# First stage of a two-layer backbone: the first quarter's modulation fetched between the fourth and the fifth token tile and summed ahead of the last tiles' transposes, with two-bank transposes

## The chip, the cores and the metric

The kernel runs on one core of one Trainium2 chip. The metric is the device time of one execution in microseconds (us); less is better. Five engines work side by side, each through its own queue in order: PE (matrix multiplication; the profile shows its weight loads apart, as PEld), DVE (vector work), ACT (activations, casts, copies), POOL (a few small operations) and SP (which here only issues transfers from main memory, HBM). Engines wait for each other by semaphores. PE writes its results into PSUM, eight banks of 512 float32 values in each of 128 partitions; everything else lies in the on-chip memory SBUF.

## What is computed

Two layers of a diffusion backbone over 512 latent tokens and 256 context tokens of width 1024. Each sub-layer begins with an RMS norm and a modulation, a shift and a scale that are computed from a conditioning vector by a large matrix; the change lies in the very first of these and in the projection behind it:

```python
sc, scc = silu(c), silu(c_ctx)
m_lat = split((sc  @ mod_w[l] + mod_b[l])[:, None, :], 6, axis=-1)
m_ctx = split((scc @ mod_w[l] + mod_b[l])[None, None, :], 6, axis=-1)
h_ctx = rms(x_ctx, norm_pre_mix[l]) * (1 + m_ctx[1]) + m_ctx[0]
h_lat = rms(x_lat, norm_pre_mix[l]) * (1 + m_lat[1]) + m_lat[0]
# layer 0: one combined projection of both streams
gq, gk, gv, gog, gz, aq, ak, av = split(concat([h_ctx, h_lat]) @ w_in, EVEN_SIZES)
```

Behind that come gated linear attention and softmax attention, an output projection, a SwiGLU network, and a second layer of another kind. The change leaves all of these as they are.

## The kernel before

Tokens are held as six tiles of 128: tiles 0 to 3 are latent, 4 and 5 context. The order is 4, 5, 0, 1, 2, 3 throughout. The 1024 features are eight blocks of 128, k = 0 to 7. For precision every matmul operand x is split in two parts, a rounded high part xH (a cast on ACT) and the rest xL (a subtraction on DVE). A product then takes three matmuls: xH with wH, xH with wL, xL with wH (`mm3`).

The first stage is in `run`, from line 1891. Its parts:

- **Tiles** (lines 1893 to 1904). For each of the six tiles: a fetch of 512 KB on SP, the sum of squares on ACT (line 676), the reciprocal root on DVE and POOL (lines 666 and 668), a scaling on DVE (line 1897), eight 128x128 transposes on PE (line 1902) and two copies out of PSUM into `xT`, one on ACT, one on DVE (line 1904). The transposes go four at a time into a one-bank PSUM tile, of which there are two (`tr_tile`).
- **Modulation.** It is worked through in four quarters, qd = 0 to 3, of two feature blocks each. `loads(qd)` (line 1913) fetches eight pieces of 256 KB of `mod_w`, and the 2 x 288 columns of the input projection that belong to this quarter, the *z weights*; the function `unit` (line 761) also casts and subtracts those weights. `sums(qd, ks)` (line 1927) multiplies the pieces with the conditioning vectors into `mod_acc`, 32 matmuls for each half of ks.
- **Apply.** `apply(qd)` (line 1943) turns the sums by a transposition on PE (`modT`), adds the bias, forms the affine numbers A and B (line 1947), applies them to `xT` (on DVE at line 1956, on ACT at line 1954) and splits the result into high and low parts (`put`, lines 734 and 735), first for the context tokens, then for the latent ones.
- **Projection.** `z(t0, qd)` (line 1959) multiplies tiles t0 and t0 + 1 with the z weights of one quarter: 12 matmuls of 288 columns. Over four quarters each z accumulates into its place in PSUM: z(4, .) and z(0, .) into a two-bank tile each (`mm_tile`, of which there are two), z(2, .) into two one-bank tiles.

The order of PE is written out by hand (lines 1976 to 1990) and kept while `self.pinned` is set: sums and apply of the first quarter, then for each further quarter the first half of its sums, the z of the quarter before, the second half of its sums, more z, apply. ACT, DVE, POOL and SP are ordered by the scheduler when the program is built, by the order in which the program names the work and by when it expects operands to be ready. At run time each queue is strictly in order.

`even_mixer` (line 1079) goes on: z(., 3) for all tiles with the evacuation on ACT (lines 1101 to 1104), then small constants, then a long list of steps (line 1219) that begins with `qk0`, the first query and key projections of the linear attention. The first `next` of `qk0` fetches, casts and subtracts its two weight units; the second issues its first matmuls (`gqk`).

Of the kernel before, what the change touches and what calls it, by code (L numbers as in the profile page):

```python
# [8 lines left out]
F32 = mybir.dt.float32  # L9
# [8 lines left out]
P = 128  # L18
# [298 lines left out]
class Net:  # L317
# [3 lines left out]
    def __init__(self, ctx, tc, I, out):  # L321
# [5 lines left out]
        self.turns, self.steps, self.pair = [], [], []  # L327
# [433 lines left out]
    def unit(self, src, k, n, pool=None, to=None):  # L761

        nc = self.nc
        raw = self.wp.tile([P, WU], F32, tag="raw", bufs=3, name="raw")
        H, L = to or [(pool or self.wp).tile([P, WU], F32R, tag=f"w{x}", bufs=4, name=f"w{x}") for x in "HL"]
        m = k * n
        rv = raw[:, :m].rearrange("p (k n) -> p k n", k=k)
        nc.sync.dma_start(out=rv, in_=src)
        nc.scalar.copy(H[:, :m], raw[:, :m])  # L769
        nc.vector.tensor_tensor(L[:, :m], raw[:, :m], H[:, :m].bitcast(F32), op=ALU.subtract)  # L770
        return H[:, :m].rearrange("p (k n) -> p k n", k=k), L[:, :m].rearrange("p (k n) -> p k n", k=k)
# [307 lines left out]
    def even_mixer(self, h, mix, z):  # L1079
# [19 lines left out]

        self.pinned = True  # L1100
        for t0 in tiles:
            for a, pt in enumerate(z(t0, 3)):
                nc.scalar.copy(zn[:, t0 + a, :], pt[:, 0:32])
                nc.scalar.copy(q_part(0)[:, t0 + a], pt[:, 32:288].rearrange("p (m e) -> p m e", m=4))
# [37 lines left out]

        gq, gk, ends = {}, {}, {}
        def qk(c):
            Ws = {x: self.unit_cols(w, x * P) for x in (c, c + 2)}
            yield
            for x in (c, c + 2):
                pt = self.mm_tile(f"gqk{x}")
                for g in groups:
                    self.gemm_T(pt, Ws[x], h, (g,))  # L1150
                    if g is groups[-1]:
                        t = gqk[x // 2] if c == 0 else mixg.tile([P, NT], F32, tag=f"gqk{x // 2}", bufs=1, name=f"gqk{x}")
                        if x < 2:
                            nc.scalar.mul(t, pt[:, :NT], 0.125)
                            gq[c] = t
                        else:
                            nc.scalar.copy(t, pt[:, :NT])
                            gk[c] = t
                    yield
# [50 lines left out]
        running = {}  # L1210
# [660 lines left out]
    def run(self):  # L1871
# [19 lines left out]
        with self.pool("pre0") as pp:  # L1891
# [85 lines left out]
            for qd in range(4):  # L1977
                loads(qd)
# [229 lines left out]
```

## Time and profile before

| | us |
|---|---|
| median of three timed runs (1678.63 to 1679.25) | 1679.15 |
| the profiled execution: its span from first to last instruction | 1679.4 |
| PE busy in it | 1639.6 |
| DVE busy | 1313.1 |
| ACT busy | 917.3 |
| first matmul of `gqk`, where the first stage ends for PE | 54.51 |

The profiled execution's span lies 0.25 us above the median. In the timeline's rows stand the start and the length of an instruction or of a merged group, the engine, the line of the kernel, the operation, what it writes and reads, how many of them, and in brackets how long its engine was idle before it and which event ended that. SPq and ACTq are the parts of an engine's queue that issue transfers. A group's length runs from its first start to its last end. Matmuls overlap in the pipeline, so the distance between two starts says more than the length of one.

### The profile page before, as it was taken

The page shows a single profiled execution, that of the slowest core. Times are in us where ns is not written, and L with a number is a line of the kernel's source. Part 1 is how long each engine was busy: PE and PEld are TensorE (multiplying, and loading weights), DVE is VectorE, ACT ScalarE, POOL GpSimd, SP SyncE. Part 2 cuts the span into 40 slices and gives each one's busy share as a digit, 9 for nine tenths or more (in the row PEclk, how much of TensorE's full clock was granted, in tenths as well). Part 3 has the DMA queues.
Part 4 walks back from the last instruction along what each step waited for, and adds up shares of the span by engine and source line. Part 5 has one row for each costly group of instructions (what it writes and reads, how often), then busy time and mean ns, then how long its engine had stood idle before and what let it go on. Part 6 is the DMA issues. An engine that isn't in the chain of part 4 may idle for free.

```text
span 1679.4 us, 32397 instructions
## 1 busy us (share of the span) xinstructions
PE 1639.6 (98%) x13347; PEld 1474.1 (88%) x13347; DVE 1313.1 (78%) x2104; ACT 917.3 (55%) x1560; POOL 122.5 (7%) x129
## 2 busy tenths in 40 slices
PE   6999998999999999999999999999999999999998
PEld 5899987888999999997887788888888899999886
DVE  4899768976898988767668648788775499987887
ACT  4745567845543443435447536566564565555564
POOL 1004110011000000002101000000000100000310
PEclk9999999999999999999999999999999999999999
DMA  9651003164243545249516542111114334433973
GB/s 330 193 156 40 2 28 101 52 213 153 85 140 101 149 146 182 76 146 211 101 57 209 189 135 64 52 53 51 52 55 159 125 103 121 118 101 101 225 164 138
DMA packets 184735, 204.77 MB, mean 122 GB/s; under 512 B 7142, under 2 KB 141836, under 8 KB 184588
## 3 DMA queue, kind: packets, MB, share of 16 engines
q1 hardware_dynamic: 173632, 181.82, 34.5%
q0 software_dynamic: 9024, 17.30, 6.0%
q10 hardware_dynamic: 1932, 3.59, 0.6%
q8 instruction: 104, 1.70, 0.4%
q14 instruction: 43, 0.35, 0.1%
HBM read 193.23 MB, written 9.46 MB: 121 GB/s over the span
## 4 chain that ended last, share of the span: by engine, by line
PE 80%; DVE 9%; DMA 4%; ACT 4%; issue 2%; POOL 1%; SPq 0%; DVEq 0%; ACTq 0%; POOLq 0%
PE nat L355 12%; PE a L355 10%; PE ff L355 8%; PE E L355 7%; PE oproj L355 6%; PE x L355 5%; PE o L355 4%; PE b L355 3%; PE D L355 3%; PE fq L355 3%; PE gqk L355 2%; PE pearly L355 2%; PE q L355 2%; PE S L355 2%; PE poh L355 1%
## 5 line engine op out<-in xcount | busy, mean ns | idle before, releaser
L355 PE MATMUL nat<-wH,x 128*128 128x256 f32 (+2 forms) x968 | 226.2, 322 | 3.1 <-ACT x L734 2.6
L355 PEld LDWEIGHTS nat<-wH,x 128*128 128x128 f32 x968 | 162.0, 190 | 21.2 <-ACT x L734 4.2
L824 ACT CAST wH<-raw 128x1024 fp32r<-128x1024 f32 x120 | 124.8, 1051 | 101.3 <-DVE raw L849 39.3
L825 DVE TENSOR_TENSOR wL<-raw,wH 128x1024 fp32r<-128x1024 f32 x120 | 145.8, 1222 | 24.2 <-ACT wH L824 23.7
L355 PE MATMUL nat<-wL,x 128*128 128x256 f32 (+2 forms) x484 | 153.5, 317 | 1.8 <-DVE wL L770 1.8
L770 DVE TENSOR_TENSOR wL<-raw,wH 128x1024 fp32r<-128x1024 f32 (+1 forms) x83 | 98.7, 1199 | 50.5 <-ACT wH L769 49.5
L355 PE MATMUL ff<-x,wH 128*128 128x512 f32 (+1 forms) x512 | 127.7, 340 | 0.0
L769 ACT CAST wH<-raw 128x1024 fp32r<-128x1024 f32 (+1 forms) x83 | 84.8, 1031 | 73.3 <-PE ff L355 19.6
L668 POOL TENSOR_TENSOR rs<-ms,neghalf 128x1 f32<-128x1 f32 (+2 forms) x62 | 64.2, 1040 | 789.7 <-DVE ms L666 789.5
L355 PE MATMUL oproj<-wH,x 128*128 128x512 f32 x320 | 102.2, 395 | 0.7 <-ACT x L1290 0.7
L355 PEld LDWEIGHTS nat<-wL,x 128*128 128x128 f32 x484 | 92.1, 190 | 7.8 <-DVE wL L770 2.7
L355 PEld LDWEIGHTS ff<-x,wH 128*128 128x128 f32 x512 | 87.3, 190 | 10.0
L597 DVE SCALAR_TENSOR_TENSOR macc<-mraw,scT,macc 128x1024 f32<-128x1024 f32 x70 | 88.0, 1282 | 10.0 <-DMA mraw<-in_mod_w_dram 9.6
L355 PE MATMUL x<-wH,two 128*128 128x512 f32 x280 | 90.7, 393 | 1.2 <-DVE y L1803 0.7
L976 ACT COPY qkh<-arr 128x512 f32<-128x512 f32 x112 | 70.1, 643 | 36.6 <-DVE arr L981 32.5
L1725 POOL DMA_DIRECT2D t<-in_ffn_w_down_dram x36 | 41.8, 1199 | 640.4 <-DVE t L1764 341.0
L355 PE MATMUL ff<-x,wL 128*128 128x256 f32 (+1 forms) x256 | 86.2, 337 | 0.0
L849 DVE TENSOR_TENSOR raw<-raw 128x512 f32<-128x512 f32 x120 | 82.8, 690 | 2.8
L981 DVE TENSOR_TENSOR arr<-arr,f 128x512 f32<-128x512 f32 x112 | 74.3, 689 | 2.1 <-ACT qkh L976 0.3
L355 PEld LDWEIGHTS oproj<-wH,x 128*128 128x128 f32 x320 | 59.9, 188 | 13.3 <-ACT x L1290 1.3
L355 PE MATMUL E<-T,wH 128*128 128x384 f32 (+1 forms) x320 | 70.4, 309 | 0.3 <-DVE go L902 0.3
L355 PE MATMUL E<-x,wH 128*128 128x384 f32 (+1 forms) x320 | 70.7, 310 | 0.0
(420 smaller groups left out, 4531.1 us busy)
## 6 DMA issues: line engine op xcount, KB each, us to landing
mraw<-in_mod_w_dram SPq DMA_DIRECT2D x80, 512.0 KB, 4.0
raw<-in_ffn_w_gate_dram SPq DMA_DIRECT2D x44, 512.0 KB, 4.9
raw<-in_ffn_w_up_dram SPq DMA_DIRECT2D x44, 512.0 KB, 4.5
raw<-in_odd_w_in_dram SPq DMA_DIRECT2D x40, 512.0 KB, 3.8
t<-in_ffn_w_down_dram POOLq DMA_DIRECT2D x30, 512.0 KB, 8.0
raw<-in_ffn_w_down_dram SPq DMA_DIRECT2D x28, 512.0 KB, 6.4
mraw<-in_mod_w_dram SPq DMA_DIRECT2D x32, 256.0 KB, 6.4
raw<-in_even_w_in_dram SPq DMA_DIRECT2D x16, 512.0 KB, 6.8
```

Source lines behind the costliest of these rows:

```text
L355: return self.pin(self.nc.tensor.matmul(*a, **k))
L597: nc.vector.scalar_tensor_tensor(a, u, w, a, op0=ALU.mult, op1=ALU.add)
L668: nc.gpsimd.tensor_tensor(rs, ms, self.neghalf.to_broadcast([P, w]), op=ALU.pow)
L769: nc.scalar.copy(H[:, :m], raw[:, :m])
L770: nc.vector.tensor_tensor(L[:, :m], raw[:, :m], H[:, :m].bitcast(F32), op=ALU.subtract)
L824: self.nc.scalar.copy(H, f)
L825: self.nc.vector.tensor_tensor(L, f, H.bitcast(F32), op=ALU.subtract)
L849: add = lambda o, x, y: nc.vector.tensor_tensor(o, x, y, op=ALU.add)
L976: nc.scalar.copy(qkv[:, :, :, half, :], dst)
L981: nc.vector.tensor_tensor(dst, dst, tb, op=ALU.mult)
L1725: add = lambda o, src: self.pin(nc.gpsimd.dma_start(out=o, in_=src, accum_op=ALU.add))
```

## The change

Four things are done in the first stage, and one behind it.

1. The tile loop becomes two functions, `fetch` and `turn`, so that the fetches can be named apart from the rest. The transposes of a tile go into one two-bank tile (`mm_tile`) instead of two one-bank tiles.
2. SP's order becomes tiles 4, 5, 0, 1, then `loads(0)`, then tiles 2, 3, then `loads(1)` to `loads(3)`. PE's written order begins with the transposes of four tiles; then come the sums of the first quarter, and the transposes of tiles 2 and 3 between the first z.
3. `unit` is cut in two: `fetched` issues the transfer and returns the function that casts and subtracts. The z weights of a quarter are now cast and subtracted by `weights(qd)`, which names them after the context half of that quarter's apply, and `behind` keeps them, on ACT and on DVE, behind the last cast and subtraction of that half.
4. `apply` is cut into `cols` (affine numbers) and `apply` for one stream and a range of tiles; in the first quarter the latent half is applied in two parts.
5. In `even_mixer` the weights of `qk0` are named ahead of the last z, behind the last cast and subtraction of the last apply; the evacuations of z on ACT are kept behind the first of these casts.

```diff
     def unit(self, src, k, n, pool=None, to=None):
+        return self.fetched(src, k, n)(pool, to)
+
+    def fetched(self, src, k, n):
         nc = self.nc
         raw = self.wp.tile([P, WU], F32, tag="raw", bufs=3, name="raw")
         m = k * n
-        nc.sync.dma_start(out=rv, in_=src)
-        nc.scalar.copy(H[:, :m], raw[:, :m])
-        nc.vector.tensor_tensor(L[:, :m], raw[:, :m], H[:, :m].bitcast(F32), op=ALU.subtract)
+        nc.sync.dma_start(out=raw[:, :m].rearrange("p (k n) -> p k n", k=k), in_=src)
+
+        def split(pool=None, to=None):
+            H, L = to or [(pool or self.wp).tile([P, WU], F32R, tag=f"w{x}", bufs=4, name=f"w{x}") for x in "HL"]
+            self.casts = self.casts[-1:] + [nc.scalar.copy(H[:, :m], raw[:, :m])]
+            nc.vector.tensor_tensor(L[:, :m], raw[:, :m], H[:, :m].bitcast(F32), op=ALU.subtract)
...
+        return split
...
+    @contextmanager
+    def behind(self):
+        with ExitStack() as s:
+            for x in self.latest:
+                s.enter_context(self.tc.issue_after(x.ins))
+            yield
...
+            def turn(t):
+                xt = xts.pop(t)
                 rs = self.rstd(self.sumsq(xt), D)
                 nc.vector.tensor_scalar(xt, xt, rs, None, op0=ALU.mult)
+                pt = self.mm_tile(f"xT{t}")
+                for k in range(KD):
+                    self.tr(pt[:, k * P : (k + 1) * P], xt[:, k * P : (k + 1) * P], self.ident)
                 for hf in range(2):
...
                     (nc.vector.tensor_copy if hf else nc.scalar.copy)(dst, src)
...
-                zu.append(self.unit(src, 2, 288))
+                zu.append(self.fetched(src, 2, 288))
...
+            def weights(qd):
+                with self.behind():
+                    zu[qd] = zu[qd]()
...
+            self.pinned = True
+            fetch(4, 5, 0, 1)
+            loads(0)
+            fetch(2, 3)
+            for qd in range(1, 4):
                 loads(qd)
-            self.pinned = True
+            for t in (4, 5, 0, 1):
+                turn(t)
             sums(0, range(8))
-            apply(0)
+            cols(0)
+            apply(0, 1, 4, 2)
+            weights(0)
+            turn(2)
+            apply(0, 0, 0, 2)
+            z(4, 0)
+            turn(3)
+            z(0, 0)
+            apply(0, 0, 2, 2)
             for qd in range(1, 4):
                 sums(qd, lo)
-                z(4, qd - 1)
-                if qd < 3:
-                    z(0, qd - 1)
+                if qd > 1:
+                    z(4, qd - 1)
+                    if qd < 3:
+                        z(0, qd - 1)
                 sums(qd, hi)
                 z(2 if qd < 3 else 0, qd - 1)
-                apply(qd)
+                cols(qd)
+                apply(qd, 1, 4, 2)
+                weights(qd)
+                apply(qd, 0, 0, 4)
             z(2, 2)
...
+        with self.behind():
+            early = qk(0)
+            next(early)
         self.pinned = True
-        for t0 in tiles:
-            for a, pt in enumerate(z(t0, 3)):
...
+        with self.tc.issue_after(self.casts[0].ins):
+            for t0 in tiles:
+                for a, pt in enumerate(z(t0, 3)):
...
```

`issue_after(x)` keeps what is named inside it behind the instruction x in x's queue; it adds no semaphore.

More of the change, by code (lines that the diff above doesn't have):

```diff
@@ L1 @@
-from contextlib import ExitStack
+from contextlib import ExitStack, contextmanager
 import concourse.bass as bass
@@ L326, in __init__ @@
         self.pinned = False
-        self.turns, self.steps, self.pair = [], [], []
+        self.turns, self.steps, self.pair, self.casts = [], [], [], []
         pool = lambda name, bufs=1, **k: ctx.enter_context(tc.tile_pool(name=name, bufs=bufs, **k))
@@ L1141, in ev_kv @@
             nc.scalar.copy(natk[:, t0 : t0 + 2, :], pt[:, :, :256])
[L1143 to L1159, printed above, removed]
         def values(c):
@@ L1209, in even_mixer @@
         att = Attention(self, natq, natk, cat)
-        running = {}
+        running = {"qk0": early}
         def run(steps):
```

62 lines of the change are left out of this document (38 added, 24 removed).

## The prediction

> **What bounds the kernel now.** The page comes first, then the busy time by stretch, then the timeline of the first stage, engine by engine. The page gives the profiled execution's span, and the view by stretch (length; busy us and instructions of PE, PEld, DVE, ACT and POOL; granted clock; DMA share; GB/s) splits its beginning.
>
> ```profile
> span 1679.4 us, 32397 instructions
> ...
> 0.00:16.00 16.00, 6.49 (x27) 5.33 (x28) 6.27 (x15) 9.72 (x17) 5.31 (x15) 1.00 0.92 324
> 16.00:36.00 20.00, 16.91 (x239) 14.01 (x237) 11.80 (x32) 9.16 (x17) 0.00 (x0) 1.00 1.10 354
> 20.36:54.51 34.15, 30.65 (x406) 26.66 (x406) 19.96 (x56) 16.58 (x37) 0.52 (x1) 1.00 0.91 281
> 54.51:219.00 164.49, 164.33 (x2310) 150.67 (x2308) 142.16 (x297) 94.91 (x186) 27.25 (x21) 1.00 0.28 85
> ```
>
> The span of 1679.4 us is 0.25 us above the median of the three timed runs, 1679.15 us. From 54.51, where the first qk matmul starts, to 219 PE is busy for 164.33 of 164.49 us. So whatever the first stage gains or loses at 54.51 is handed on whole: up to 219 PE has no gap that could take it up. Behind 219 PE waits now and then for DVE and ACT, whose work there follows from PE's own; I take the shift to pass through these waits too, which no row here proves. The stage itself is loose: 30.65 of 34.15 us. The change touches only what lies before 54.51, so the question is when the matmul that now stands at 54.51 will start. In PE's timeline (start, us, instruction, idle time before it and its releaser) the turning points of the stage are:
>
> ```profile
> 8.08 1.91 PE L358 MATMUL xT<-ident,xt 128*128 128x128 f32 x8
> 16.88 1.10 PE L358 MATMUL xT<-ident,xt 128*128 128x128 f32 x8 [0.27 <-DVE xT L1904]
> 20.36 1.96 PE L355 MATMUL mod_acc<-mraw,scT 128*32 128x128 f32 x64
> 24.97 0.40 PE L355 MATMUL nat<-wH,x 128*128 128x288 f32 x1 [0.84 <-ACT x L734]
> 31.27 0.27 PE L358 MATMUL modT<-ident,modrows 128*128 128x128 f32 x1
> 33.33 0.40 PE L355 MATMUL nat<-wH,x 128*128 128x288 f32 x1 [0.78 <-ACT x L734]
> 37.38 1.08 PE L355 MATMUL mod_acc<-mraw,scT 128*32 128x128 f32 x32
> 38.39 0.40 PE L355 MATMUL nat<-wH,x 128*128 128x288 f32 x1
> 38.63 0.30 PE L355 MATMUL nat<-wL,x 128*128 128x288 f32 x1
> 40.10 0.27 PE L358 MATMUL modT<-ident,modrows 128*128 128x128 f32 x1
> 42.16 0.40 PE L355 MATMUL nat<-wH,x 128*128 128x288 f32 x1 [0.78 <-ACT x L734]
> 44.14 1.08 PE L355 MATMUL mod_acc<-mraw,scT 128*32 128x128 f32 x32
> 46.86 0.27 PE L358 MATMUL modT<-ident,modrows 128*128 128x128 f32 x1
> 48.92 0.40 PE L355 MATMUL nat<-wH,x 128*128 128x288 f32 x1 [0.21 <-ACT x L734]
> 54.51 0.71 PE L355 MATMUL gqk<-x,wH 128*128 128x512 f32 x2
> ```
>
> Eight transposes take 1.91 us early and 1.10 us later. The first quarter's modulation sums (mod_acc) start at 20.36 and take 1.96. One z, a pair of tiles in one quarter, is 12 matmuls: from 38.39 to the transposition modT at 40.10, 1.71 us, of which 1.47 follow the start of its second matmul at 38.63 (the first that reads wL). Half a quarter's sums take 1.01 (37.38 to 38.39). I use three marks: M1, M2 and M3, the ends of the modT of the second, third and fourth quarters: 31.54, 40.37 and 47.13. What PE then waits for is ACT's first cast of x (the brackets at 33.33 and 42.16: 0.78 us each).
>
> ```profile
> 11.86 0.68 DVE L1904 COPY xT<-xT 128x512 f32<-128x512 f32 x1
> 23.55 0.17 DVE L1947 SCALAR_TENSOR_TENSOR aff<-modcol,col 128x4 f32<-128x4 f32 x1
> 26.18 0.67 ACT L769 CAST wH<-raw 128x576 fp32r<-128x576 f32 x1
> 31.97 0.17 DVE L1947 SCALAR_TENSOR_TENSOR aff<-modcol,col 128x4 f32<-128x4 f32 x1
> 32.17 0.81 ACT L1954 ACTIVATE xT<-xT,modcol,aff 128x512 f32<-128x512 f32 x1 [5.33 <-DVE aff L1947]
> 32.89 1.22 ACT L734 CAST x<-xT 128x256 fp32r<-128x256 f32 x3
> L770 DVE TENSOR_TENSOR wL<-raw,wH 128x576 fp32r<-128x576 f32 x4 | 3.0, 751 | 0.0
> ```
>
> These are ACT's and DVE's rows. The quarter's affine numbers are ready at 23.72 in the first quarter and at 32.14 in the second, 0.60 after M1. ACT first runs a latent activation (0.81), then the three casts (1.22 for two context casts and one latent one). The cast of the z weights for the second quarter (0.67, and 0.75 for DVE's part) stands at 26.18, 7 us ahead of the z that reads it (33.33), in time that nobody waits for.
>
> **The change, part by part.**
>
> *Transfers.* The order on SP becomes four tiles, the first quarter's modulation, its z weights, two tiles, the rest.
>
> ```profile
> mraw<-in_mod_w_dram SPq DMA_DIRECT2D x32, 256.0 KB, 6.4
> xt<-in_x_dram SPq DMA_DIRECT2D x4, 512.0 KB, 5.6
> raw<-in_even_w_in_dram SPq DMA_DIRECT2D x4, 288.0 KB
> ```
>
> The count of bytes is the same. By the rates above (324 GB/s to 16 us, 354 after) 5.18 MB are in by 16 us. Four tiles and eight blocks of 256 KB are 4.2 MB: in by about 13.2 instead of 16.2. The fifth tile (0.52 MB) follows at about 15.5, with 0.3 MB of z weights ahead of it, the sixth at 17.0, and everything after that lands when it did: the second quarter at about 23, the fourth at about 37 (12.5 MB). No later sum comes to wait for it, as the first wants its data after 23 and the last after 40.
>
> *First quarter.* Now the sums stand behind four tiles' transposes, not six. Turn 4 still runs at 8.08 to 9.99, turn 5 follows to 11.9 without a wait, as there are two double banks. Turn 0 needs the first one back, so it waits for DVE's copy that ends at 12.54; at the early pace it ends at 14.5, turn 1 at 15.6 to 16.4; I take 16.0. The sums add 1.96: 18.0. From sums to affine it takes 1.40 (22.32 to 23.72), so the affine numbers stand at **A = 19.4** instead of 23.72. Ends: 17.5, if the copy comes right behind its transposes and the rest runs at 1.10; 21.2, if the sums run at the early pace too.
>
> From A the two context casts and, held behind them now, the weights' cast and subtraction have to run. In the second quarter's rows the context casts end 1.35 after the affine numbers (32.14, activation, 32.89, two of three casts); with the shorter first activation I take 1.05. With 0.67 and 0.75 behind, the second matmul of z(4, 0) starts at A + 2.5. Meanwhile the fifth tile is normalised:
>
> ```profile
> L676 ACT ACTIVATE junk<-xt 128x1024 bf16<-128x1024 f32 x6 | 6.3, 1057 | 3.2 <-DMA xt<-in_ctx_dram 2.7 <-DMA xt<-in_x_dram 0.4
> L676 ACT ACTIVATION_READ_ACCUMULATOR junk<-xt 128x1 f32 x6 | 1.1, 188 | 0.0
> L666 DVE TENSOR_SCALAR ms<-ss 128x1 f32<-128x1 f32 x6 | 0.9, 150 | 7.4 <-ACT junk L676 7.4
> L668 POOL TENSOR_TENSOR rs<-ms,neghalf 128x1 f32<-128x1 f32 x6 | 4.3, 717 | 9.6 <-DVE ms L666 9.4
> L1897 DVE TENSOR_SCALAR xt<-xt,rs 128x1024 f32<-128x1024 f32 x6 | 4.5, 752 | 1.9 <-POOL rs L668 1.9
> ```
>
> 1.06 + 0.19 + 0.15 + 0.72 + 0.75 = 2.87 us from its landing at 15.5 to its transposes. They stand behind the first modT in PE's order, so at about 18.7 to 19.8; ACT is idle from 15.5 to A but for copies, and they hide ahead of z(4, 0). The sixth tile's do not: PE's order is fixed, and after z(4, 0) (1.47) come its transposes (1.10), then a wait of 0.75 that is new: z(0, 0) takes the double bank that those transposes filled, so DVE's 0.68 copy has to end first, z(4, 0) holding the other. Then z(0, 0) 1.71, both halves of the second sums 2.0, z(2, 0) 1.71, modT 0.27: 9.0 in all. M1 = A + 2.5 + 9.0 = **30.9, 0.6 earlier** than 31.54. Of 4.3 us gained at A, 1.4 are spent waiting on weights, and 2.9 on transposes, their copy and a half of sums that stood ahead of z before. By A's ends it is from 2.5 earlier to 1.2 later.
>
> *Other quarters.* The weights' cast is held behind the second context cast on ACT, its subtraction behind DVE's. That is a new wait. Queued behind it on ACT are the latent casts, on DVE their subtractions. After M: 0.60 to the affine numbers, 1.35 to the end of the context casts, 0.67, 0.75: the second z matmul at M + 3.4, z's end at M + 4.9.
> - Second quarter: z(0, 1) adds 1.71, so the sums that stood at 37.38 (M1 + 5.84) stand at M1 + 6.6: 0.75 later.
> - Third: the sums at 44.14 (M2 + 3.77) stand at M2 + 4.9: 1.1 later.
> - Fourth: z(0, 3) and z(2, 3) behind, so 54.51 (M3 + 7.38) becomes M3 + 8.3: 0.9 later.
>
> Sum: **2.75 later**. Nothing in before shows this queue, so both ends: if ACT takes the context casts ahead of the latent activation, each loses 0.4 less (1.5 in all); if a latent cast (0.6) goes first, 0.6 more (4.5). I take the middle, since the rows show activation, context, latent.
>
> *qk weights and evacuations.* The casts of the first qk weights now stand behind the last latent cast, and z's evacuations on ACT behind the first of them.
>
> ```profile
> L769 ACT CAST wH<-raw 128x1024 fp32r<-128x1024 f32 x2 | 2.1, 1052 | 0.0
> L770 DVE TENSOR_TENSOR wL<-raw,wH 128x1024 fp32r<-128x1024 f32 x1 | 1.2, 1215 | 0.0
> 47.21 10.37 SPq L461 DMA_DIRECT2D mraw<-in_mod_w_dram  x4
> 110.67 1.28 DVE L537 SCALAR_TENSOR_TENSOR macc<-mraw,scT,macc 128x1024 f32<-128x1024 f32 x1
> 114.99 1.06 PE L355 MATMUL mod_acc<-macc,one 128*32 128x512 f32 x8
> ```
>
> 1.05 and 1.22 are hidden by z(0, 3) and z(2, 3), 3.4 us of PE; without that cover 2.3 at most. The z weights' raw buffers come free later, so on SP two fetches of value weights, and behind them perhaps the next modulation's at 47.21, go out later. That modulation is summed on DVE to 111.95 and read by PE at 114.99: 3.0 us of slack, and more if PE comes later. I cost it at nothing; beyond the slack it would cost what the fetch is late by. The first quarter's latent half split in two adds short operations beside z(4, 0): nothing.
>
> [...] The profile grants PE a clock of 1.00 in every stretch, yet the same eight transposes take 1.91 us at 8.08 and 1.10 at 16.88: PE is slow at first and turns fast somewhere between. [...]
>
> Sum: 1679.4 - 0.6 + 2.75 = 1681.5 in the profiled execution, 0.25 less beside the median: **1681.3 us**. Ends: -2.5 + 1.5 = -1.0 and 1.2 + 4.5 = +5.7.
>
> **The rivals.**
> - **R1, slower: the fifth tile queues behind the weights on ACT.** ACT's order is a plan made ahead. If it puts that tile's sum of squares behind the weights' cast (A + 1.7 = 21.1), its transposes start 2.87 later, at 24.0, and z(4, 0) at 25.1, ends at 26.8; by the forecast it ended at 23.4. 3.4 more: 1684.7. It decides from 17.9 on: up to there the transposes are out of the way when the weights are. For it: the landing (15.5) and the casts are near each other. Against it: the slow transposes put A behind 17.5 in any case.
> - **R2, the front gain outweighs the waits.** Turns run promptly and fast (A = 17.5, -2.5) and the quarters cost 1.5 to 2.2: 0.3 to 1.0 faster, 1678.5. If the weights also slip in at no cost, 1676.6; it would take another 0.8 from somewhere to get under 1675.8. For it: before, these casts never held PE. Against it: they now cannot start before the affine numbers.
> - **R3, PE falls back to its slow pace** in the gaps between sums, turn 2 and z(4, 0): 1.91 / 1.10 on z(4, 0), turn 3 and z(0, 0) (4.5 us) adds 3.3: 1684.6. [...]
> - **R4, the change does nothing**: the scheduler's order or the transfers give the same 54.51. Transfers don't bind, so little: 1679.2.
>
> **How the numbers follow.** Forecast 0.47 (1679.8 to 1682.5 on its own), R1 0.19, R2 0.21, R3 0.07, R4 0.06. About 0.2% (3.4 us) is what a measurement can tell from no change. Forecast, R4 and most of R2 lie within it; R1 and R3 nearly all beyond it; of R2 0.06 beyond it on the fast side, for sizes that I have wrong. So faster 0.06, same 0.69, slower 0.25. The range goes from inside R2 to past R1: 1677.4 to 1685.2.
>
> **What would show it.** Right: sums near 16 to 18; the fifth tile's sum of squares before the first context cast; the weights' casts between context and latent casts in each quarter, with PE waiting on DVE's wL at each z(4, q); the sixth tile's transposes between z(4, 0) and z(0, 0) with a wait on the copy; first qk matmul near 56.6. Wrong: weights' casts early, or ACT starting the second context cast long before M + 1.7; first qk before 54; a gap on PE behind 56, which would break the handing-on.

## The result, and the profile after

The changed kernel takes **1694.18 us** (median of 4 runs, 1691.42 to 1697.02), the kernel before 1679.2 beside it (4 runs, 1678.63 to 1680.59): ratio 1.009, 95% interval 1.0076 to 1.0105. It is 15 us slower; the prediction was 1681.3, with a range up to 1685.2.

The page of the changed kernel begins:

```profile
span 1690.5 us, 32401 instructions
...
PE 1640.4 (97%) x13347; PEld 1477.7 (87%) x13347; DVE 1313.6 (78%) x2107; ACT 918.4 (54%) x1563; POOL 123.5 (7%) x129
```

PE has as much work as before (1640.4 us, 1639.6 before) and more waiting. Where it waits shows in where the same matmuls start:

| | before | after | later by |
|---|---|---|---|
| first quarter's sums begin | 20.36 | 14.53 | -5.8 |
| M1 | 31.54 | 33.15 | 1.6 |
| M2 | 40.37 | 42.89 | 2.5 |
| M3 | 47.13 | 51.00 | 3.9 |
| first `gqk` | 54.51 | 63.51 | 9.0 |
| first `oproj`, the output projection | 338.7 | 348.1 | 9.4 |
| first `a` (the feed-forward part that follows `pearly`) | 450.3 | 464.2 | 13.9 |
| first `fq`, in the second layer | 1004.2 | 1015.8 | 11.6 |
| end of the span | 1679.4 | 1690.5 | 11.1 |

Of the 13.9 us that are lost by `a`, 9.0 come ahead of `gqk` (3.9 of them up to M3) and 4.5 between `oproj` and `a`, a place that the prediction never looked at. In PE's timeline the first stage now reads (start, us, instruction, idle time before it and what ended that):

```profile
14.53 1.95 PE L355 MATMUL mod_acc<-mraw,scT 128*32 128x128 f32 x64
...
20.98 1.87 PE L358 MATMUL xT<-ident,xt 128*128 128x128 f32 x8 [3.75 <-DVE xt L1922]
...
25.06 1.03 PE L358 MATMUL xT<-ident,xt 128*128 128x128 f32 x8
27.50 0.40 PE L355 MATMUL nat<-wH,x 128*128 128x288 f32 x1 [1.40 <-DVE xT L1929]
...
32.88 0.27 PE L358 MATMUL modT<-ident,modrows 128*128 128x128 f32 x1
...
35.86 0.40 PE L355 MATMUL nat<-wH,x 128*128 128x288 f32 x1 [1.70 <-ACT wH L774]
36.66 0.40 PE L355 MATMUL nat<-wL,x 128*128 128x288 f32 x1 [0.39 <-DVE wL L775]
...
45.56 0.40 PE L355 MATMUL nat<-wH,x 128*128 128x288 f32 x1 [1.66 <-ACT wH L774]
...
53.67 0.40 PE L355 MATMUL nat<-wH,x 128*128 128x288 f32 x1 [1.08 <-ACT wH L774]
...
63.38 0.27 PE L358 MATMUL pt_rows<-ident,rows 86*128 86x86 f32 x1 [2.47 <-DMA mraw<-in_mod_w_dram]
63.51 0.71 PE L355 MATMUL gqk<-x,wH 128*128 128x512 f32 x2
```

Four things are to be seen. The fifth tile's transposes at 20.98 wait 3.75 us, for its scaling on DVE. The z at 35.86, 45.56 and 53.67 wait for wH and then for wL, as forecast. The transposition of the late constants' rows (`pt_rows`) at 63.38, for which nobody waited before, now holds `gqk` for 2.47. And the same eight transposes take 1.87 at 20.98 and 1.03 at 25.06. The view by stretch (length, PE busy, granted clock, DMA share, GB/s) shows why, here in pieces of some 3.5 us:

```profile
17.50:20.98 3.48, 0.00 (x0) 1.00 1.10 351
20.98:24.60 3.62, 3.62 (x17) 0.53 1.10 357
51.60:55.10 3.50, 2.03 (x13) 1.00 0.00 0
55.10:58.60 3.50, 3.50 (x17) 0.52 0.87 272
424.20:427.60 3.40, 0.58 (x3) 0.95 1.09 305
427.60:431.00 3.40, 3.39 (x11) 0.55 1.07 326
```

The clock that PE is granted falls to 0.52 to 0.55 three times, each time for some 3.5 us straight behind a piece in which PE was busy for 0.00, 2.03 and 0.58 us. In the kernel before it is 1.00 up to 1675 and falls only there (0.53 from 1675 to the end), when PE has no matmul left. Each of these slow spells costs about half its length, 1.5 to 1.7 us: an estimate from the clocks and lengths of the rows at 20.98, 55.10 and 427.60.

The third lies far behind the change, at `pearly`, the first matmuls of the feed-forward part. First the changed kernel (PE, then DVE), then the kernel before:

```profile
424.40 0.39 PE L355 MATMUL oproj<-wH,x 128*128 128x512 f32 x1
427.61 1.01 PE L355 MATMUL pearly<-b,wH 128*128 128x384 f32 x2 [2.82 <-DVE ms L666]
```

```profile
426.33 1.22 DVE L746 TENSOR_TENSOR pn<-oproj,gv 128x1024 f32<-128x1024 f32 x1
```

```profile
415.02 0.39 PE L355 MATMUL oproj<-wH,x 128*128 128x512 f32 x1
415.25 0.51 PE L355 MATMUL pearly<-b,wH 128*128 128x384 f32 x2
```

```profile
416.96 1.22 DVE L746 TENSOR_TENSOR pn<-oproj,gv 128x1024 f32<-128x1024 f32 x1
```

Before, `pearly` followed the last `oproj` matmul at once, while DVE read that `oproj` tile (`pn`) 1.7 us later. Now `pearly` starts only when DVE has read it (426.33 + 1.22). The order of the instructions is the same there. What differs is the place in PSUM, as the built programs have it (first bank of each tile):

```
               last oproj tile   first pearly tile
before         6                 2
changed        2                 2
```

The two-bank tiles of the first stage's pool used to be asked for behind the single ones and got banks 4 to 7. The two-bank transposes ask for them first, so they get 2 to 5, and all later two-bank tiles of this pool with them.

### The profile page after: what moved, and what is told of

The parts are those of the page before. It is cut to its first block, busy times and chain, and to the rows that moved or that the text cites. A ratio compares the mean times of both kernels' runs of the same rounds, so it can differ in the third digit from the quotient of the medians.

```text
span 1690.5 us, 32401 instructions
## 1 busy us (share of the span) xinstructions
PE 1640.4 (97%) x13347; PEld 1477.7 (87%) x13347; DVE 1313.6 (78%) x2107; ACT 918.4 (54%) x1563; POOL 123.5 (7%) x129
## 4 chain that ended last, share of the span: by engine, by line
PE 84%; DVE 7%; ACT 3%; DMA 3%; issue 2%; POOL 1%; ACTq 0%; DVEq 0%; SPq 0%; POOLq 0%
PE nat L355 13%; PE a L355 11%; PE ff L355 8%; PE E L355 8%; PE x L355 6%; PE oproj L355 6%; PE o L355 4%; PE b L355 4%; PE D L355 4%; PE pearly L355 3%; PE fq L355 3%; PE q L355 2%; PE S L355 2%; PE gqk L355 2%; PE poh L355 1%
## 5 line engine op out<-in xcount | busy, mean ns | idle before, releaser
L355 PE MATMUL b<-x,wH 128*128 128x384 f32 (+1 forms) x320 | 70.6, 310 | 0.0
```

The source lines that it names most:

```text
L355: return self.pin(self.nc.tensor.matmul(*a, **k))
```

## The experiments

Theories at the start: three parts of the change each cost by themselves (places in PSUM; z weights cast late; `gqk`'s weights and the evacuations behind them), and the front does besides. The rival: everything behind the first stage is only a consequence of its lateness.

**E1, the places put back.** In the changed kernel:

```diff
+            self.sc_tile("pre", 0), self.sc_tile("pre", 1)
             fetch(4, 5, 0, 1)
```

> The changed kernel, with the two single PSUM banks of sc0 and sc1 reserved ahead of the first two-bank tile of the first stage, so that the stage's two-bank tiles lie in banks 4 to 7 again and the last oproj tile no longer in bank 2; nothing else changes. Bank theory: the first feed-forward no longer waits for that tile's evacuation. The first pearly matmul follows the last oproj matmul with under 0.5 us of waiting instead of 2.82, the slow-clock spell behind it (427.6 to 430.9 in the changed kernel) is gone, the marks up to oproj stay within 0.5 us of the changed kernel's, and the end comes 2.8 to 4.4 earlier: 1687 to 1690 against a mean of 1694 (a spell elsewhere can add 1.6). Rival, the late start itself (all of the mixing stage runs some 9 us later than the transfers and the modulation it meets): the wait of 2.8 stays and the time is within 1.5 us of the changed kernel's.

1688.86 us (1687.81 to 1690.83), 1.006 (1.0045 to 1.0075). PE's timeline there:

```profile
427.10 0.39 PE L355 MATMUL oproj<-wH,x 128*128 128x512 f32 x1
427.32 0.51 PE L355 MATMUL pearly<-b,wH 128*128 128x384 f32 x2
```

The wait is gone and so is the spell, although `oproj` starts even later (350.8). The time is 5.3 below the changed kernel's. Miss: the first stage, unchanged, came 2.9 later at `gqk` in this profile, with a further spell at 47.5 to 51 (pairs of z matmuls take 0.68 there, 0.43 elsewhere). The spells differ from run to run.

**E2, z weights not held back.** For the 2nd to 4th quarter `zu[qd] = zu[qd]()` ahead of `cols(qd)`, instead of `weights(qd)` behind the context's apply.

> The changed kernel, with the casts of the 2nd to 4th quarter's z weights not held back behind the context's casts, as before the change; the first quarter's are as changed. Cast theory: z(4,1), z(4,2) and z(4,3) no longer wait for wH (1.70, 1.66 and 1.08 us in the changed kernel) and less for wL; the steps from the first mark to the second and to the third get 1.0 to 2.0 us shorter each (6.76 and 5.12 to the sums' ends), the slow spell at 55 goes with the waits, and the first gqk matmul comes 3.0 to 5.5 us earlier than at 63.5; the time is 2 to 5 us below the changed kernel's if the rest hands it on. Rival, ScalarE as a whole is what binds (the casts only change places with the context's and the tokens' casts): z(4,q) waits for the context's x instead, and gqk comes under 1.5 us earlier.

1692.48 (1691.77 to 1693.21), 1.0082 (1.0065 to 1.0099). No wait for wH is left, but `z(4, 2)` now waits 1.45 us for x, and M1 to M3 is 17.33 instead of 17.85. That looks like the rival, but the edit had put wL on DVE ahead of the context's applies, where the kernel before doesn't have it. E8 repeats it properly.

**E3, `gqk`'s weights asked for late again.** Part 5 of the change undone:

```diff
-        with self.behind():
-            early = qk(0)
-            next(early)
         self.pinned = True
-        with self.tc.issue_after(self.casts[0].ins):
-            for t0 in tiles:
+        for t0 in tiles:
...
-        running = {"qk0": early}
+        running = {}
...
```

> The changed kernel, with the weights of the first gqk (casts and fetches) not asked for ahead of z's evacuations and these evacuations not held behind them: this part is as before the change. Queue theory: the late constants' transfers are issued some 2 to 3 us earlier against the last z matmul, the wait of 2.47 us ahead of the transposition of the late rows (63.38 in the changed kernel) shrinks to under 0.7, and gqk comes 1.5 to 2.5 us earlier. Rival, the edit does what it looks like (gqk's weights are ready sooner): without it, gqk waits for its own casts instead, and its start is within 0.7 us of 63.5 or later.

1694.47 (1693.17 to 1695.2), 1.0091 (1.0076 to 1.0106): no gain. The wait for the rows is gone, as the queue theory said, but `gqk` waits for its own casts:

```profile
64.50 0.74 PE L355 MATMUL gqk<-x,wH 128*128 128x512 f32 x2 [1.42 <-ACT wH L774]
66.39 0.50 PE L355 MATMUL gqk<-x,wL 128*128 128x512 f32 x1 [1.15 <-DVE wL L775]
```

Alone, this part costs nothing, as the rival said: one wait takes the other's place. In the kernel before, the first of these casts ran at 43.94, ahead of the last quarter. Here, with the z weights late, it runs at 63.39.

**E4, the kernel before with the two-bank tag asked for first** (`self.mm_tile("pre")` ahead of the tiles, and each `oproj` pair in reverse).

> The kernel before, with nothing changed but the places in PSUM: the two-bank tag is asked for ahead of the single banks of the first stage, and each pair of oproj tiles takes its two places in the other order, so that the last oproj tile lies in bank 2, as in the changed kernel. All instructions and their order on every engine are those of before. Bank theory: up to the end of oproj the marks are those of before within 0.5 us, then the first pearly matmul (no wait in the kernel before) waits 2.5 to 3.2 us, with or without a slow spell of 1.6 behind it; the time is 1681 to 1684. Rival, the late start: no such wait, and 1678.5 to 1680.5.

1678.46 (1677.79 to 1680.55), 0.9999 (0.9989 to 1.0008). No wait at `pearly`, but the edit doesn't make the conflict: the built program has the last `oproj` tile in bank 4, not in 2 as its expectation says. What it shows is that the tag's place alone costs nothing, and how far one kernel's profiles differ: here M1 is at 33.45 and `gqk` at 56.45, 1.9 later than in the profile before, with the same instructions and a span that is 0.7 shorter.

**E5, the conflict in the kernel before.** One tile of six is turned through a two-bank tile, so the two places alternate the other way and the last `oproj` tile lies in bank 2:

```diff
+                two = self.mm_tile(f"xT{t}") if t == 3 else None
                 for hf in range(2):
-                    pt = self.tr_tile(f"xT{t}{hf}")
+                    pt = two[:, 512 * hf : 512 * hf + 512] if t == 3 else self.tr_tile(f"xT{t}{hf}")
```

> The kernel before, with one of its six token tiles (the last, tile 3) turned through one two-bank tile instead of two single ones; nothing else. This puts the two-bank tag ahead of the single banks and shifts the alternation of its two places by one, so that the last oproj tile lies in bank 2, the place of the first pearly tile, as in the changed kernel (the run before this one put the tag there, but the last oproj tile in bank 4, so it did not make the conflict). Bank theory: the first pearly matmul, with no wait in the kernel before, waits 2.5 to 3.2 us for VectorE's reading of the last oproj tile, with or without a slow spell of 1.7 behind it. Of such lateness at 425 part is absorbed by 795 (the run before this one: 2.4 us late at oproj, nothing at 795), so the time is 1679 to 1683. Rival, the wait comes from the late start: no wait at pearly.

1687.64 (1686.68 to 1691.19), 1.0055 (1.004 to 1.007).

```profile
423.01 0.39 PE L355 MATMUL oproj<-wH,x 128*128 128x512 f32 x1
426.22 0.62 PE L355 MATMUL pearly<-b,wH 128*128 128x384 f32 x2 [2.82 <-DVE ms L666]
```

The same wait, 2.82 to the hundredth, in a kernel that has of the change one two-bank turn only. **The places theory stands.** The time rose by more than forecast because a second thing came along: the scheduler, planning anew, put the cast of `gqk`'s first weights behind z's evacuations (55.78 instead of 43.94). `gqk` waits 0.83 and 2.09 for them, and a long slow spell follows (59 to 66; clock 0.50 from 60 to 64). Another stands at 24 to 28 (0.59), in the first stage.

**E6, the front alone.** E1's and E3's edits, and the z weights cast a quarter ahead, behind the token casts, where the kernel before has them:

```diff
             apply(0, 0, 2, 2)
+            weights(1)
...
                 apply(qd, 1, 4, 2)
-                weights(qd)
                 apply(qd, 0, 0, 4)
+                if qd < 3:
+                    weights(qd + 1)
```

> The changed kernel with three parts as before the change: the places in PSUM, the qk weights asked for after z's evacuations, and the z weights of the 2nd to 4th quarter cast a quarter ahead, behind the quarter's token casts. What is left of the change is the front: first quarter fetched and summed ahead of the last two token tiles. By the sum of parts: first mark at 33 to 35 (before: 31.5 to 33.5), the stretch from the first mark to the third 15.6 plus or minus 0.4 (before 15.59, changed 17.85), from the third to gqk 7.4 plus or minus 0.6 (before 7.38, changed 12.51), gqk at 56 to 58.5, no wait at pearly, and a time of 1679 to 1682. Rival, the late parts are a consequence of the front (the transfers and ScalarE run behind by then): the stretches stay within 0.8 us of the changed kernel's and the time is above 1686.

1683.43 (9 runs, 1681.07 to 1686.28), 1.0028 (1.0018 to 1.0037). M1 34.03; M1 to M3 15.62; M3 to `gqk` 8.40 (forecast 7.4, 0.6 either way); no wait at `pearly`. So the rival falls: the late parts are not a consequence of the front. But the time is above the range given: the front itself costs 4.6.

**E7, PE kept busy.** In the changed kernel:

```diff
+            def warm(n):
+                pt = self.tr_tile("warm")
+                for _ in range(n):
+                    self.tr(pt[:, :P], self.ident, self.ident)
...
+            warm(24)
             turn(2)
```

and 9 ahead of `z(0, 0)`, 13 ahead of `z(4, 1)` and of `z(4, 2)`, 8 ahead of `z(4, 3)`.

> The changed kernel, with idle transpositions of the identity (24, 9, 13, 13 and 8 of some 0.13 us, their results unread) put on TensorE where it waits in the first stage: ahead of the turning of tile 2, ahead of z(0,0), ahead of z(4,1), z(4,2) and z(4,3). They feed nothing and wait for nothing but PSUM. Clock theory: the slow spells at 21 to 25 and at 55 to 59 come from the waits ahead of them; with TensorE busy there both are gone (PEclk 1.00 up to 62), the waits' ends stay where they are, turn 2 takes 1.1 instead of 1.87, gqk starts 2.5 to 3.5 us earlier against the first modT than the 46.6 of the changed kernel, and the time is 2 to 4 below the changed kernel's. Rival, the clock has other reasons: the spells stay, or come somewhere else before 62, and gqk is within 1 us.

1693.87 (1692.79 to 1695.96), 1.0089 (1.0074 to 1.0104). The slow spells up to 62 go, as the clock theory said; the gain doesn't arrive. Up to 62 the clock is 1.00 throughout, turn 2 takes 1.06, and M1 comes 15.29 behind the first modT instead of 16.25. But `gqk` starts 45.97 behind it, not 43 to 44:

```profile
58.89 0.24 ACTq L405 DMA_DIRECT2D rows<-in_hgrn_out_norm_dram  x1
```

```profile
63.12 0.27 PE L358 MATMUL pt_rows<-ident,rows 86*128 86x86 f32 x1 [4.27 <-DMA mraw<-in_mod_w_dram]
```

```profile
58.70:62.20 3.50, 0.15 (x2) 1.00 1.05 383
62.20:65.60 3.40, 2.48 (x7) 0.69 0.97 338
```

ACT issues the last piece of the rows at 58.89, 2.07 earlier than in the changed kernel (60.96), and yet `pt_rows` starts only 0.26 earlier: here 4.23 us lie between issue and use, at a DMA share of 1.05, where it had been 2.42. And behind the longer wait a new slow spell begins at 63.

**E8, z weights cast a quarter ahead**, in the changed kernel, with E6's diff alone.

> The changed kernel, with the z weights of the 2nd to 4th quarter cast a quarter ahead, behind the quarter's token casts, as before the change (the run with these casts not held back put their VectorE half ahead of the context's applies, which the kernel before does not do). Cast theory: no wait for wH at z(4,1) to z(4,3); from the first mark to the third 15.6 plus or minus 0.4 us instead of 17.85; the late rows' wait stays, since gqk's part is as changed; time 2 to 4 us below the changed kernel's. Rival, ScalarE binds as a whole: the stretch stays above 17.

1691.6 (1690.94 to 1692.32), 1.0075 (1.0058 to 1.0092), 2.6 below the changed kernel. M1 to M3 is 15.62; at the first z of the second quarter PE waits as it did before the change:

```profile
36.78 0.40 PE L355 MATMUL nat<-wH,x 128*128 128x288 f32 x1 [0.81 <-ACT x L734]
```

The cast theory stands, with the size that the prediction gave. The late rows' wait stays, as forecast, and is longer than in the changed kernel: 3.74.

**E9, what a delay is worth.** The kernel before, with 32 idle transpositions ahead of the first `gqk`.

> The kernel before, with 32 idle transpositions of the identity (some 0.13 us each, unread) put on TensorE straight ahead of the first gqk matmul: everything behind the first stage starts 4.2 us later, and nothing else is changed. Hand-on theory (the assumption of the prediction): the delay arrives whole, 1682.5 to 1683.5 against 1678.8 for before. Rival, absorption: the stretch between the first down-projection groups (a, at 450) and q (at 795) waits for transfers that don't move with TensorE and takes back up to 2.4 us, as the marks of the earlier runs say (the bank-map run: 2.5 us late at a, nothing at q): the delay is 3.9 to 4.4 at a, 1.5 to 2.2 at q, and the time 1680 to 1681.

1685.06 (7 runs, 1681.95 to 1686.79), 1.003 (1.0018 to 1.0041). `gqk` starts at 58.25, 3.74 later; the interval puts the loss at 3.0 to 6.9. The delay arrives whole: in the profile it is 4.1 at `a` and 4.7 at `q`, where the rival had 1.5 to 2.2, so the rival falls. The time is above the forecast of 1682.5 to 1683.5; why it rose by more than the delay isn't shown.

**E10, places and z weights put back, `gqk`'s part as changed.**

> The changed kernel, with two of its parts as before the change: the places in PSUM, and the z weights cast a quarter ahead. Against the front-only run, gqk's weights are still asked for ahead of z's evacuations, and these held behind them. By the differences so far (5.3 for the places, 2.6 for the weights) 1686.3. If the gqk part costs something by itself once the weights are cast in time: 2 to 4 above the front-only run's 1683.4, with a wait for the late rows of 2 to 4 us ahead of gqk, which starts 3 us or more later against the third mark than the 8.4 of the front-only run. Rival, it costs nothing (alone, undoing it was worth nothing): within 1 of 1683.4.

1687.5 (1684.39 to 1688.39), 1.0048 (1.0033 to 1.0063), 4.1 above E6. ACT's issue of the rows, then PE:

```profile
53.77 2.00 ACT L774 CAST wH<-raw 128x1024 fp32r<-128x1024 f32 x2
...
57.48 0.24 ACTq L405 DMA_DIRECT2D rows<-in_hgrn_out_norm_dram  x1
```

```profile
61.67 0.38 PE L358 MATMUL pt_rows<-ident,rows 86*128 86x86 f32 x1 [4.23 <-issue]
```

Two casts of `gqk`'s weights (2.00), then six pairs of evacuations, then the issue at 57.48, and `pt_rows` waits 4.23. A slow spell follows, from 60.5 to 67.5 (clock 0.50 from 62 to 66). In E6 that issue stands at 53.30, the wait is 0.44, and no such spell follows (1.00 from 54 to 70). So this part costs some 4 us once the z weights are cast in time, and nothing while they are late (E3).

**E11, the front alone with PE kept busy**: E6 with 24 idle transpositions ahead of turn 2 and 9 ahead of `z(0, 0)`.

> The front-only run, with idle transpositions of the identity on TensorE (24 ahead of the turning of tile 2, 9 ahead of z(0,0), unread). Clock theory: the slow spell at 18 to 26 goes, the first mark is 15.0 to 15.4 us behind the first modT instead of 17.0, gqk comes 1.5 to 2 us earlier and so does the first half; at the end 0.5 to 2 are left of it, 1681.5 to 1683. Rival, the front's cost is not the clock's: the first mark comes no earlier, time as the front-only run's.

1684.1 (10 runs, 1680.83 to 1689.15), 1.0032 (1.0022 to 1.0042). No slow spell in the profile up to 1676 (clock 1.00), M1 15.29 behind the first modT, `gqk` 2.3 earlier than in E6 (55.77), and no gain in the time.

**E12, the same with half of the second quarter's sums ahead of `z(0, 0)`.**

> The same, with the first half of the second quarter's sums (4 of its 8 steps) put ahead of z(0,0), into the wait for VectorE's copy of tile 3, instead of the 9 idle transpositions there. The first mark is another 0.8 to 1.1 us earlier, 14.0 to 14.5 behind the first modT and so some 31.5, as in the kernel before; the rest as in the run before this one. If the front can gain at all, this is where: the time is 1678.5 to 1681, the same as before's 1678.8 at best. Rival, the transfers of the second quarter land too late for it, and the sums wait: no better than the run before this one.

1682.7 (10 runs, 1680.76 to 1685.17), 1.0024 (1.0014 to 1.0033). M1 is 14.41 behind the first modT, as forecast. The time is still 3.9 above before's.

**E13, two-bank transposes alone**, in the kernel before, with the single banks reserved first.

> The kernel before, with all six tiles turned through two-bank tiles, and the single banks reserved first, so that the places in PSUM of everything behind the first stage are those of before. By the one-tile run (1687.6, with the conflict at pearly of 2.8 and its spell of 1.7, and with gqk waiting 0.8 and 2.1 for its weights and a long spell there): without the conflict, 4.5 less, 1683.1, if ScalarE's order again has the cast of gqk's first weights behind z's evacuations, which the kernel before has ahead of the last quarter; gqk then waits 2 to 3 us for its weights, a slow spell follows, and pearly waits for nothing. Rival, the whole cost of the one-tile run was the conflict: 1678.5 to 1680.5.

1680.62 (10 runs, 1678.78 to 1682.03), 1.0007 (0.9998 to 1.0017): no loss that this measurement can tell. No wait at `pearly`, and here the scheduler left the cast of `gqk`'s first weights where it had been. ACT in E13, then in E5:

```profile
44.16 1.04 ACT L769 CAST wH<-raw 128x1024 fp32r<-128x1024 f32 x1
```

```profile
55.78 1.06 ACT L769 CAST wH<-raw 128x1024 fp32r<-128x1024 f32 x1
```

That leaves nothing visible for the two-bank turns themselves, so E5's 9 us are put down to the conflict and this cast together. No run moves the cast alone.

**E14, the order of the front alone**: E6's edits, with two one-bank tiles for each turn.

> The front-only run, with the tiles turned through two single banks each, as before the change: what is left is the order of the front alone. If the two-bank turning is what the front costs: z(0,0) no longer waits 1.4 us for VectorE's copy of tile 3, the first mark is 1 to 2 us nearer to the first modT than the 17.0 of the front-only run, and the time is 1680 to 1682 against 1683.4. Rival, the order itself costs it (TensorE waits 3.8 us for tile 2, then turns it and z(4,0) at the slow clock, whichever bank): within 1 of 1683.4.

1681.34 (10 runs, 1680.01 to 1684.46), 1.0015 (1.0005 to 1.0024). `z(0, 0)` follows turn 3 without a wait. M1 is 13.31 behind the first modT, but that itself comes 2.94 later (19.94), so M1 is only 0.8 earlier than in E6. There is no slow spell ahead of `gqk` (clock 1.00), though PE waits 2.17 for the fifth tile. The two-bank turning costs some 2 us in this order, and the order itself some 2.2.

**What the parts cost**, taken away one after another (medians; the range of single runs is 3 to 6 us, so each step is good to a microsecond or two):

| | us | step |
|---|---|---|
| changed kernel | 1694.2 | |
| places in PSUM put back (E1) | 1688.9 | 5.3 |
| and z weights a quarter ahead (E10) | 1687.5 | 1.4 |
| and `gqk`'s weights after the evacuations (E6) | 1683.4 | 4.1 |
| and one-bank transposes (E14) | 1681.3 | 2.1 |
| the kernel before (beside E14) | 1679.2 | 2.2 |

Taken from the changed kernel itself, the z weights were worth 2.6 (E8) and `gqk`'s weights nothing (E3): the parts don't simply add up. No version tried beats the kernel before.

## Why the prediction was wrong, point by point

- **Handed on whole.** Right, and now shown by E9 where it had been assumed. The 2.8 that the two profiles seem to take back between `a` and the end (13.9 to 11.1) looks like a difference between executions rather than absorption: before's profile has 2.05 us of waits between 440 and 800 (PE busy 357.95 of 360), the changed kernel's 0.61 from 450 to 812 (361.39 of 362). Being late doesn't take these waits away: E9, 3.74 late at `gqk`, has 2.70 of them (357.30 of 360).
- **The time base.** Misread by 2 us, but the forecast itself doesn't suffer, as its 2.15 ends up added to the median. The prediction took the profiled span as the time, 0.25 above the median. A run's time is some 1.8 above its span (1692.25 for the span of 1690.5; 1680.55 for 1678.7 in E4), so the profile of before should be an execution of some 1681.2. That, and the changed kernel's profile being one of its quicker runs, is why the profiles differ by 11.1 and the medians by 15.
- **First quarter: 0.6 earlier; in fact 1.6 later.** The affine numbers came at 17.82, near the early end (17.5). The step that failed is the second matmul of z(4, 0) at A + 2.5, with the fifth tile's transposes hidden ahead of it. The tile's chain on ACT, DVE and POOL:

```profile
16.73 1.06 ACT L676 ACTIVATE junk<-xt 128x1024 bf16<-128x1024 f32 x1 [1.50 <-DMA xt<-in_x_dram]
```

```profile
18.51 0.14 DVE L666 TENSOR_SCALAR ms<-ss 128x1 f32<-128x1 f32 x1
...
20.08 0.75 DVE L1922 TENSOR_SCALAR xt<-xt,rs 128x1024 f32<-128x1024 f32 x1 [0.44 <-POOL rs L668]
```

```profile
18.80 1.25 POOL L668 TENSOR_TENSOR rs<-ms,neghalf 128x1 f32<-128x1 f32 x1 [7.60 <-DVE ms L666]
22.04 0.55 POOL L668 TENSOR_TENSOR rs<-ms,neghalf 128x1 f32<-128x1 f32 x1 [2.00 <-DVE ms L666]
```

  It landed at 16.7, not 15.5; its small step on DVE stood behind the quarter's first applies, which had become ready (18.51; ACT was done at 17.88); and POOL's root, begun while DVE was at work, took 1.25 instead of 0.72. So its transposes began at 20.98 (18.7 to 19.8 in the sum), on a PE that had idled for 3.75 and now ran at a granted clock of 0.53, and the second z matmul at A + 5.1. The z weights' subtraction, too, stood behind the tile's scaling on DVE and ended at 21.50, A + 3.7, so A + 2.5 wouldn't have been met without the transposes either. The new wait for the copy was 1.40, not 0.75, because the two copies out of one two-bank tile ran one behind the other:

```profile
26.14 0.58 ACT L1929 COPY xT<-xT 128x512 f32<-128x512 f32 x1 [2.35 <-PE xT L358]
```

```profile
26.75 0.69 DVE L1929 COPY xT<-xT 128x512 f32<-128x512 f32 x1 [2.22 <-ACT xT L1929]
```

  In the kernel before DVE's copy waits for PE alone (17.58, 19.02 and 20.47, 0.75 each). A larger head start at A made the gap on PE wider, not the end earlier. One sum of the prediction is off besides: of the 4.3 us gained at A it has 1.4 and 2.9 spent, all of it, and yet 0.6 left; by its own rows 1.0 and 2.7 are spent.
- **Other quarters: 2.75 later.** Right. The sums stand at M1 + 6.8 and M2 + 5.1 (6.6 and 4.9 in the sum), the last z ends at M3 + 9.9, of which some 1.7 are a slow spell (by its 0.52 over 3.50 us; 8.3 in the sum). M1 to M3 gives 2.3 of it, and E8 takes just these back (2.6 in the time; 1.4 for the same edit in E10 against E1).
- **`gqk`'s weights and the evacuations: costed at nothing.** Wrong: 4.1 in E10 against E6. The cover named there (z(0, 3) and z(2, 3)) hides the casts. What was missed are the transfers that ACT itself issues behind the evacuations. The prediction counted SP's queue, not ACT's: the last piece of the rows went from 50.46 to 60.96, against M3 from 3.3 to 10.0, and PE needs it ahead of `gqk`.
- **Two-bank transposes: given no term at all but a wait for a copy.** Wrong, 5.3 by E1. Most of their price is not where they run (2.1 in the new order by E14, nothing visible in the old one by E13). They moved every two-bank tile of the pool in PSUM, and the one at `oproj` met the next pool's first tile.
- **R3, the slow pace: 0.07.** It came, and was under-weighted. That PE falls back to a slow pace was the author's estimate: no row of before shows it, they have PE slow at first only. From the end of the sums to the fifth tile's transposes the prediction has 0.7 to 1.8 us (18.0 to 18.7 or 19.8); it was 4.5 (16.48 to 20.98), 3.75 of it idle behind modT, and then the granted clock was 0.53: turn 2 took 1.87 and z(4, 0) was slow for most of its length (matmul pairs of 0.68, then 0.42), while turn 3 (1.03) and z(0, 0) were not. Nor are the spells tied to that place: others stand behind waits of 2.82 at `pearly` and of 1.08 + 0.40 at `z(4, 3)`. Each of the three lasted 3.4 to 3.6 us at 0.52 to 0.55. What brings one on isn't shown: PE was busy for 0.00 of 3.48 us ahead of the first, for 2.03 of 3.50 us ahead of the second.
- **R1** didn't happen as told: the sum of squares ran ahead of the weights' cast (16.73 and 18.98). But it had the right tile: the fifth did hold z(4, 0), by way of DVE and POOL. R2's early A came (17.82 for 17.5), its gain didn't. R4 is out.

**Open:** of the front's 4.6, some 2 us go with the two-bank turning (E14). But E11 and E12 have M1 where the kernel before has it (31.9 and 33.0; 31.5 to 33.5 in the five profiles with the old order) and lose 4 to 5 us all the same. M3 to `gqk` takes 8.2 to 8.6 there instead of 7.4, `gqk` to `a` 397.6 to 398.0 instead of 395.8. Most of the second difference is one wait, which the kernel before's profile doesn't have. In E11, then in E12 (us in total, times, longest):

```profile
PE logit L355 <- DVE lb L446: 1.5, 1, 1.5
```

```profile
PE logit L355 <- DVE lb L446: 1.3, 1, 1.3
```

E6 has 0.9 of it, E14 0.7, E4 0.4. `lb` is made on DVE from the late constants, behind the cast of `masks_f`, another transfer that ACT issues: DVE stands at that cast until 57.96 in E11, 6.3 us behind the issue, and in the kernel before until 54.98, 4.2 behind it. No run takes this wait away, and the rest wasn't followed further.

## What to carry to other kernels

A change to the first stage of a pooled kernel can move tiles in PSUM for everything behind it (here the last `oproj` tile from bank 6 to 2, 5.3 us by E1): compare the places of the tiles at each border between pools, not only the order of instructions. When work is pushed behind other work on an engine, list the transfers that this engine issues too, and who waits for them. A gap of one or two microseconds on PE can cost more than itself: here waits of 1.08 + 0.40 and of 2.82 us were each followed by a slow spell, 1.5 to 1.7 us more by the estimate above. But look first at whether the next thing PE needs is ready sooner when the gap is filled: in E7 `pt_rows` came only 0.26 earlier, behind a wait of 4.27, and the time stayed (1693.87 for 1694.18).

## What was not expected of the hardware

- Slow spells of 3.4 to 3.6 us at a clock of 0.52 to 0.55 (in E6 one from 18.3 to 25.5, twice as long, mean clock 0.57) came behind pieces in which PE was only partly idle, too. In E5 it is a piece with 1.98 of 3.40 us busy (clock 0.60 in the next 3.40); the kernel before, with 2.82 of 3.40 busy there, has none (1.00). But not every nearly idle piece was followed by one: in E14 PE was busy for 0.83 of the 3.40 us from 18.90, and the clock stayed at 1.00. They come in different numbers in different runs: two stretches ahead of `gqk` in the changed kernel, three in E1 with the same work (by the matmul pairs of 0.68).
- The granted clock doesn't show the slow start: in the kernel before, eight transposes take 1.91 us at 8.08 at a recorded clock of 1.00.
- POOL's root (`rs`) took 0.55 us where it began while DVE was idle (12.75 and 14.89 in the kernel before), also after 8.31 us of idling (414.43 in the changed kernel). Begun during an operation of DVE, it ended some 0.4 us behind DVE's work: 1.02 at 7.29 (to 8.31, DVE to 7.89), 1.25 at 18.80 (to 20.05, DVE to 19.64). The kernel before and E6 show the same at 7.26 and 18.90. Not every operation of DVE went with a longer root: at 379.16 it took 0.56 beside `pn`, which reads from PSUM (1.22 from 379.00).
- The last piece of the rows, 0.5 KB, was used 2.42 us after its issue in the changed kernel (DMA share 1.03), 4.23 after it in E7 (1.05) and 4.19 after it in E10 (1.03 to 1.07), with PE idle in between.
